# The four column-group matmuls of a product kept as one piece by a list scheduler

## The chip, the cores and the metric

The kernel runs on one core of one Trainium2 chip. The metric is the device time of one execution in microseconds (us), the median of several runs of the same built program.

## What is computed

One step of a hybrid decoder layer for two request groups that share weights: a prompt of 2048 tokens and eight decode tokens, each token a row of 1024 channels. Cut to what matters here:

```python
x = x + parallel_mixer(rms_norm(x, norm_mix), ...)       # convolution module and gated DeltaNet
x = x + memory_attend(rms_norm(x, norm_mem_q), mem_k, mem_v, w_mq, w_mo)
x = x + swiglu(rms_norm(x, norm_ffn), w_gate, w_up, w_down)
...
def memory_attend(h, mem_k, mem_v, w_mq, w_mo):
    q = (h @ w_mq).reshape(bsz, seq, MEM_HEADS, MEM_HD)
    s = jnp.einsum('blhd,bmhd->bhlm', q, mem_k) * (MEM_HD ** -0.5)
    pr = jax.nn.softmax(s, axis=-1)
    o = jnp.einsum('bhlm,bmhd->blhd', pr, mem_v)
    return o.reshape(bsz, seq, MEM_HEADS * MEM_HD) @ w_mo
```

The decode tokens have their own cached keys and values (8 tokens, 256 memory rows, 4 heads of 256). Everything is float32.

## The kernel before, in words

The prompt is worked in four blocks of 512 tokens: the mixer for all blocks first, then for each block the output projection, the memory attention (`sc` scores, `pr` probabilities, `rg` result) and the feed-forward part, whose products are `fx`, `fy`, `fz` (gate and up) and `dx`, `dy`, `dz`, `dn` (down). These prompt products use operands split into a high and a low part in float32r, three matmuls for each product, and fill TensorE's whole width of 128 columns.

The eight decode tokens ride along. Three of their products have few columns on the stationary side, 8 or 32, and are written in float32 without a split. Each of these matmuls writes 8 or 32 partitions of a PSUM bank, starting at partition 32 j, and so uses one of TensorE's four column groups; the helper `quad` issues one. Four of them with j = 0 to 3, on four different operands, make a group:

- `dr` (in `dec_rows`): a decode row times `w_mq` (operand `hdn`) or `w_mo` (operand `hcat`). The four stationary operands are four channel chunks of the row, the four moving ones four weight tiles `raw`, 128x512, loaded by DMA. A product of 512 columns takes two groups, each weight four: 8 groups, 32 matmuls.
- `podd` (in `dec_attend`): the probabilities `pb` times the cached values. The four moving operands are `vtd` tiles, two tokens by two halves of the memory rows. Two column halves with four groups each: 8 groups, 32 matmuls.

The decode scores come before that: a DVE or POOL multiplication `kt` = `kt` * `qb` and a DVE reduction into `scs`, 32 of each, while the prompt's third block is in its attention.

**What sets the order.** The program is first recorded: every engine call is put on a tape with its operands (`Tape.add`). `Tape.order` then makes the order in which the calls are issued, by list scheduling. It keeps a clock for each engine and for the DMA; `cost` gives each call a duration, `LAT` the delay between engines. `graph` finds for each call what it must follow (`preds`): who wrote its operands, who used its output before, and for PE the last PE call on the same PSUM tile. At each turn, the engine that is free first takes, among the calls that are ready by its clock, the one with the smallest key. For PE the key is the place on the tape; for the others it is the smallest key of what hangs on them (`keys`). A matmul with a later place is therefore taken when nothing earlier is ready at that moment, and the next turn chooses again. `tensor_tensor` calls in SBUF can go to DVE or POOL, whichever the planner finds free.

So in the kernel before, each of the four `quad` calls of a group is a call of its own: it is ready when its own operand has landed by the planner's clock and the call before it on the same bank is issued, and it competes with the `fx`, `fy` and `fz` rows for its turn. The planner's cost of one is `n * 0.4492 + 15` ns.

All calls of the tape are issued from one line (515 before, 530 after), so the profile tells them apart by tile names alone.

Of the kernel before, what the change touches and what calls it, by code (L numbers as in the profile page):

```python
# [8 lines left out]
F32 = mybir.dt.float32  # L9
# [71 lines left out]
class Clock:  # L81


    def __init__(self):
        self.at = {"pe": 0.0, "act": 0.0, "dve": 0.0, "pool": 0.0, "sp": 0.0, "dma": 0.0}
        self.ready, self.used = {}, {}
        self.table = None
        self.ring, self.nbank = {}, {"mm": 3, "s": 3, "o": 1, "cv": 1}
        self.held = set()
# [23 lines left out]
def elems(ap):  # L113
    n = 1
    for x in ap.shape[1:]:
        n *= x
    return n
# [37 lines left out]
class Tape:  # L155
# [10 lines left out]

    def __init__(self):
        self.ops, self.tag_of, self.bufs, self.psum = [], {}, {}, set()
        self.real, self.other, self.given = {}, {}, {}

    def pool(self, pool, bufs, psum=False):
        return TapePool(self, pool, bufs, psum)
# [16 lines left out]
    def cost(self, eng, op, args, kw, outs, ins):  # L189

        n = max(elems(a) for a in outs + ins) if ins else elems(outs[0])
        psum_in = any(a.name in self.psum for a in ins)
        if eng == "pe":
            m = elems(args[1])
            n = elems(args[2])
            if op == "transpose":
                return max(n, m) * 0.835 + 3, False, None
            if args[1].dtype == F32 and m <= 32 and n >= 256:
                return n * 0.4492 + 15, False, None
            if args[1].dtype == F32:  # L200
                return 2 * (max(max(m, 64) * 0.835, 2 * n * 0.4492) + 3), False, None
            return max(max(m, 64) * 0.835, (n if n >= 256 else 4 * n) * 0.4492) + 3, False, None
        if eng == "sp":
            size = 4
            for x in outs[0].shape:
                size *= x
            return max(size / 295.0, 90.0), False, None
        if eng == "act":
            ptr = len(ins) - 1
            return 0.834 * n + (50 if psum_in else 94) + 93 * ptr + (92 if "accum_out" in kw else 0), False, SETS.get(kw.get("func"))  # L210
        big = sum(a.name not in self.psum and elems(a) > 1 for a in ins)
        if eng == "dve":
            ptr = any(hasattr(kw.get(k), "shape") for k in ("scalar", "scalar1"))
            half = op in ("tensor_copy", "tensor_scalar") and not psum_in
            shared = big > 1 or (half and n > 2 and not any(a.name in self.psum for a in outs))
            return 68 + (61 if ptr else 0) + n * (6.2 if op == "reciprocal" else 0.525 if half else 1.042), shared, None
        if kw.get("op") == ALU.pow:
            return 280 + 180 * n, True, None
        if op in ("memset", "affine_select"):
            return 40 + 0.85 * n, False, None  # L220
        return 150 + n * (2.15 if op == "tensor_tensor" else 3.4), True, None

    def box(self, a):

        if a.name in self.psum:
            return 0, 0, 0, 0
        dims = a.ap
        shape = a.tensor.shape
        pitch = 1
        for x in shape[1:]:  # L230
            pitch *= x
        if a.space == bass.MemoryType.DRAM:
            pitch = shape[-1]
        r0, c0 = a.offset // pitch, a.offset % pitch
        r1, c1 = r0, c0
        for st, n in dims:
            if pitch > 1 and st % pitch == 0:
                r1 += st // pitch * (n - 1)
            else:
                c1 += st * (n - 1)  # L240
        if c1 >= pitch:
            r1, c0, c1 = r1 + c1 // pitch, 0, pitch - 1
        return r0, r1, c0, c1

    def graph(self):

        writes, reads, last_pe = {}, {}, {}
        preds, tiles = [], []
        over = lambda x, y: x[0] <= y[1] and y[0] <= x[1] and x[2] <= y[3] and y[2] <= x[3]
        inside = lambda x, y: y[0] <= x[0] and x[1] <= y[1] and y[2] <= x[2] and x[3] <= y[3]  # L250
        for n, (eng, op, _, args, _, outs, ins, _) in enumerate(self.ops):
            p = {}
            for a in ins:
                if a.name in self.tag_of:
                    b = self.box(a)
                    for k, x in writes.get(a.name, ()):
                        if over(b, x):
                            p[k] = 1
            for a in outs:
                if a.name in self.tag_of:  # L260
                    b = self.box(a)
                    for k, x in writes.get(a.name, ()):
                        if over(b, x):
                            p[k] = 1
                    for k, x in reads.get(a.name, ()):
                        if over(b, x):
                            p[k] = 1
                    if eng == "pe":
                        if a.name in last_pe:
                            p[last_pe[a.name]] = 1  # L270
                        last_pe[a.name] = n
            for a in outs:
                if a.name in self.tag_of:
                    b = self.box(a)
                    for d in (writes, reads):
                        d[a.name] = [(k, x) for k, x in d.get(a.name, ()) if not inside(x, b)]
                    writes[a.name].append((n, b))
            for a in ins:
                if a.name in self.tag_of:
                    reads.setdefault(a.name, []).append((n, self.box(a)))  # L280
            p.pop(n, None)
            preds.append(list(p))
            tiles.append(list(dict.fromkeys(a.name for a in outs + ins if a.name in self.tag_of)))
        return preds, tiles

    def keys(self, succs, line, first, tiles):


        N = len(self.ops)
        nxt = {}  # L290
        for tag, ts in line.items():
            for k, t in enumerate(ts[: -self.bufs[tag]]):
                nxt[t] = first[ts[k + self.bufs[tag]]]
        key = list(range(N))
        for n in range(N - 1, -1, -1):
            if self.ops[n][0] != "pe":
                after = [key[m] for m in succs[n]] + [key[nxt[t]] for t in tiles[n] if t in nxt and nxt[t] > n]
                key[n] = min([n + LATER, *after])
        return key

    def order(self):
# [69 lines left out]
        def taken(t):  # L371
            load = max(0.0, clock["dve"] - t)
            for _, m in avail["dve"]:
                if not gone[m]:
                    load += cost(m, "dve")[0]
            return load
# [11 lines left out]
        while len(done) < N:  # L388
# [20 lines left out]
            while av:  # L409
# [4 lines left out]
                if not busy and n in self.other:  # L414
                    load += cost(n, "dve")[0]
                    busy = load > BACKLOG
                    n = None
                    continue
# [14 lines left out]
                if stop is None:  # L433
                    if e == "dve" and cost(n, e)[1] and port_at > t + 150 and not skipped:

                        other = [(k2, m) for k2, m in av if not gone[m] and not cost(m, e)[1] and all(x in given for x in tiles[m]) and bank_at(m, e) <= t]
                        if other:
                            skipped.append((k, n))
                            k, n = min(other)
                            av.remove((k, n))  # L440
                            heapify(av)
                            new = []
                    break
# [194 lines left out]
def hybrid_step(ctx: ExitStack, tc: tile.TileContext, i: dict, o: list):  # L638
# [146 lines left out]
    class Plan(list):  # L785
# [21 lines left out]
        def extend(self, keys):  # L807
            for key in keys:
                self.append(key)
# [2321 lines left out]
```

## Time and profile before

| | |
|---|---|
| median of 3 runs | 2936.22 us (2935.59 to 2937.78) |
| profiled execution, its own time | 2932.24 us |
| its span, first to last instruction | 2930.5 us |
| mean granted TensorE clock | 0.998 |
| busy: PE, DVE, ACT, POOL | 2890.9, 2470.0, 1452.0, 754.0 us |
| DMA moved | 569.40 MB, 194 GB/s |

How to read the rows that follow in the prediction. A row of the groups gives engine, operation, output <- inputs, the shape of the stationary operand (partitions * columns), the output's shape, the number of records, then busy time in us, the mean of one in ns, and the idle time of the engine just before them. A row of the timeline gives start and length in us, then the same names; records of one kind that follow each other are merged, with their count; brackets hold an idle time before the row. The length reaches to the end of the last record, which overlaps the next start, so what a row takes from the engine is the difference of two starts. A float32 matmul leaves two records. A row of waits gives who waited for whom, us in total, times, and the longest. A row of windows gives the stretch, its length, the busy time of PE, weight loads, DVE, ACT and POOL, the granted clock, the DMA share and GB/s.

### The profile page before, as it was taken

How to read it: one execution, taken by the hardware profiler on the slowest of the kernel's cores; microseconds unless marked ns; L12 is line 12 of the kernel's file. 1: busy time of each engine (PE TensorE's matmuls, PEld its weight loads, DVE VectorE, ACT ScalarE, POOL GpSimd, SP SyncE). 2: the span in 40 equal slices, each digit the busy share in tenths (PEclk: the TensorE clock that was granted, in tenths of full speed). 3: DMA queues.
4: the chain of work that ended last, by engine and by line, in shares of the span. 5: the costliest groups of instructions: out<-in, count | busy, mean ns of one | idle time of the engine just before them, and what ended most of it. 6: DMA issues, size and time to landing. Idle time of an engine off the chain costs nothing.

```text
span 2930.5 us, 55769 instructions
## 1 busy us (share of the span) xinstructions
PE 2890.9 (99%) x19620; PEld 2598.0 (89%) x19620; DVE 2470.0 (84%) x5364; ACT 1452.0 (50%) x3034; POOL 754.0 (26%) x850
## 2 busy tenths in 40 slices
PE   9999999999999999999999999999999999999998
PEld 8999878888888887989888789999888999999998
DVE  8868988999978897978888877788867888888888
ACT  7544545555664445545454443344444444444444
POOL 3211342553313034613201810000542232410000
PEclk9999999999999999999999999999999999999999
DMA  6533435777774334866677767777636666666664
GB/s 222 155 97 105 128 115 162 228 247 258 225 243 124 119 102 133 261 192 201 213 259 251 246 217 246 232 232 238 201 102 207 210 214 199 209 230 197 214 209 131
DMA packets 363032, 569.40 MB, mean 194 GB/s; under 512 B 55840, under 2 KB 158560, under 8 KB 362736
## 3 DMA queue, kind: packets, MB, share of 16 engines
q1 hardware_dynamic: 362752, 565.84, 60.3%
q8 instruction: 155, 2.54, 0.3%
q14 instruction: 125, 1.02, 0.1%
HBM read 457.77 MB, written 108.51 MB: 193 GB/s over the span
## 4 chain that ended last, share of the span: by engine, by line
PE 51%; DVE 2%; DMA 2%; ACT 1%; issue 1%; POOL 0%; SPq 0%; POOLq 0%; DVEq 0%; ACTq 0%
PE fy L515 11%; PE fz L515 8%; PE fx L515 7%; PE rg L515 6%; PE dx L515 5%; PE dn L515 5%; PE dz L515 3%; PE sc L515 3%; PE dy L515 1%; DMA w<-sums 1%; DVE w L515 1%; PE pu L515 0%; PE podd L515 0%; DVE x L515 0%; PE pch L515 0%
## 5 line engine op out<-in xcount | busy, mean ns | idle before, releaser
L515 ACT ACTIVATE w<-raw 128x512 fp32r<-128x512 f32 (+1 forms) x1066 | 649.5, 619 | 888.9 <-issue 138.2
L515 DVE TENSOR_TENSOR w<-raw,w 128x512 fp32r<-128x512 f32 (+1 forms) x861 | 610.8, 713 | 161.5 <-ACT w L515 156.8
L515 PE MATMUL fy<-op,w 128*128 128x256 f32 (+1 forms) x3168 | 434.3, 282 | 0.1
L515 PEld LDWEIGHTS fy<-op,w 128*128 128x128 f32 x3168 | 399.1, 188 | 7.6 <-issue 1.8
L515 PE MATMUL hd<-hT,w 128*128 128x512 f32 (+2 forms) x1920 | 394.2, 356 | 1.0 <-DVE hT L515 0.5
L515 POOL TENSOR_TENSOR w<-raw,w 128x512 fp32r<-128x512 f32 (+1 forms) x205 | 282.5, 1382 | 341.7 <-ACT w L515 277.9
L515 DVE SCALAR_TENSOR_TENSOR cacc<-cu,cw,cacc 128x512 f32<-128x512 f32 x480 | 357.6, 745 | 9.2 <-ACT cacc L515 5.7
L515 PEld LDWEIGHTS hd<-hT,w 128*128 128x128 f32 x1920 | 302.6, 188 | 45.4 <-ACT w L515 1.2
L515 PE MATMUL fx<-op,w 128*128 128x256 f32 (+1 forms) x2112 | 297.3, 283 | 0.3
L515 PE MATMUL fz<-op,w 128*128 128x256 f32 (+1 forms) x2112 | 285.8, 283 | 1.8 <-DMA w<-sums 1.7
L515 PEld LDWEIGHTS fx<-op,w 128*128 128x128 f32 x2112 | 269.4, 189 | 8.3 <-ACT w L515 3.4
L515 PEld LDWEIGHTS fz<-op,w 128*128 128x128 f32 x2112 | 264.5, 188 | 9.0 <-issue 4.8
L515 PE MATMUL dx<-fo,w 128*128 128x256 f32 (+1 forms) x1344 | 197.8, 283 | 0.7 <-DVE x L515 0.6
L515 PE MATMUL rg<-pT,w 128*128 128x512 f32 x768 | 191.3, 400 | 2.1 <-ACT pr L515 0.9
L515 PE MATMUL dn<-ff,w 128*128 128x512 f32 (+2 forms) x960 | 192.0, 353 | 0.3 <-ACT ffs L515 0.2
L515 PE MATMUL sc<-w,hT 128*128 128x512 f32 x768 | 188.5, 399 | 3.6 <-ACT pr L515 3.6
L515 PE MATMUL rg<-catS,w 128*128 128x512 f32 (+2 forms) x960 | 186.2, 351 | 0.0
L515 PEld LDWEIGHTS dx<-fo,w 128*128 128x128 f32 x1344 | 174.7, 188 | 2.7 <-DVE x L515 1.3
L515 PEld LDWEIGHTS rg<-catS,w 128*128 128x128 f32 x960 | 154.6, 188 | 24.6
L515 PEld LDWEIGHTS sc<-w,hT 128*128 128x128 f32 x768 | 141.4, 188 | 36.8 <-ACT pr L515 5.9
L515 PEld LDWEIGHTS rg<-pT,w 128*128 128x128 f32 x768 | 140.5, 188 | 35.8 <-ACT pr L515 2.2
L515 PEld LDWEIGHTS dn<-ff,w 128*128 128x128 f32 x960 | 150.9, 188 | 22.0 <-DVE ffs L515 0.5
(421 smaller groups left out, 4836.6 us busy)
## 6 DMA issues: line engine op xcount, KB each, us to landing
w<-sums SPq DMA_DIRECT2D x222, 512.0 KB, 4.4
raw<-in_w_gate_dram SPq DMA_DIRECT2D x192, 256.0 KB, 3.5
sums<-w SPq DMA_DIRECT2D x66, 512.0 KB, 3.7
raw<-in_w_up_dram SPq DMA_DIRECT2D x118, 256.0 KB, 3.4
raw<-in_w_down_dram SPq DMA_DIRECT2D x224, 128.0 KB, 2.8
raw<-in_w_in_dram SPq DMA_DIRECT2D x96, 256.0 KB, 3.2
raw<-sums SPq DMA_DIRECT2D x74, 256.0 KB, 3.3
raw<-wk SPq DMA_DIRECT2D x64, 256.0 KB, 2.8
```

The source lines that it names most:

```text
L515: fn(*args, **kw)
```

## The change

The scheduler is told of the groups. A new function `quarter` says which PE calls are column-group matmuls (float32, at most 32 stationary columns, at least 256 moving ones). In `graph`, up to four such calls in a row on the same PSUM tile are a group: the first call of a group is given what the other three must follow too, so it isn't ready before all four operands are. In `keys`, the second to fourth have the length of the tape taken from their keys, so that, ready as soon as the one before is issued, they come ahead of everything else. The planner's cost of one such matmul rises from `n * 0.4492 + 15` to `n * 0.4492 + 38` ns. No instruction of the computation is added or removed; only the order changes, and with it which of DVE and POOL makes some sums.

```diff
@@ __init__ @@
-        self.real, self.other, self.given = {}, {}, {}
+        self.real, self.other, self.given, self.follow = {}, {}, {}, set()
@@ cost @@
-            if args[1].dtype == F32 and m <= 32 and n >= 256:
-                return n * 0.4492 + 15, False, None
+            if self.quarter(op, args):
+                return n * 0.4492 + 38, False, None
@@
+    def quarter(self, op, args):
+
+        return op == "matmul" and args[1].dtype == F32 and elems(args[1]) <= 32 and elems(args[2]) >= 256
@@ graph @@
-        preds, tiles = [], []
+        preds, tiles, group = [], [], []
...
             p.pop(n, None)
+            if eng == "pe" and self.quarter(op, args):
+                if group and group[0] == outs[0].name and len(group) < 5:
+                    preds[group[1]] = list(dict.fromkeys([*preds[group[1]], *(k for k in p if k < group[1])]))
+                    group.append(n)
+                    self.follow.add(n)
+                else:
+                    group = [outs[0].name, n]
+            elif eng == "pe":
+                group = []
             preds.append(list(p))
@@ keys @@
+        for n in self.follow:
+            key[n] -= N
         return key
```

What it does to the order is shown at three places. The first is PE in the feed-forward part of the second block, where the last group of the second `w_mq` product stands; `dr_3367` is its bank, `raw_...` the weight tiles, `fy` and `fx` rows of the prompt. Before:

```order
L515 MATMUL dr_3367_3566<-raw_3392_3591,hdn_104 8x512
L515 MATMUL dr_3367_3566<-raw_3393_3592,hdn_104 8x512
L515 MATMUL dr_3367_3566<-raw_3394_3593,hdn_104 8x512
L515 MATMUL fy_3401_3600<-op_2433_2632,w_3403_3602 128x256 x3
L515 MATMUL fy_3401_3600<-op_2445_2644,w_3403_3602 128x256 x3
L515 MATMUL fy_3401_3600<-op_2459_2658,w_3403_3602 128x256 x3
L515 MATMUL fy_3401_3600<-op_2482_2681,w_3403_3602 128x256 x3
L515 MATMUL dr_3367_3566<-raw_3395_3594,hdn_104 8x512
L515 MATMUL fx_3411_3610<-op_2430_2629,w_3410_3609 128x256 x6
```

After:

```order
L530 MATMUL dr_3367_3566<-raw_3392_3591,hdn_104 8x512
L530 MATMUL dr_3367_3566<-raw_3393_3592,hdn_104 8x512
L530 MATMUL dr_3367_3566<-raw_3394_3593,hdn_104 8x512
L530 MATMUL dr_3367_3566<-raw_3395_3594,hdn_104 8x512
L530 MATMUL fy_3401_3600<-op_2433_2632,w_3403_3602 128x256 x3
L530 MATMUL fy_3401_3600<-op_2445_2644,w_3403_3602 128x256 x3
L530 MATMUL fy_3401_3600<-op_2459_2658,w_3403_3602 128x256 x3
L530 MATMUL fy_3401_3600<-op_2482_2681,w_3403_3602 128x256 x3
L530 MATMUL fx_3411_3610<-op_2430_2629,w_3410_3609 128x256 x6
```

The fourth matmul has moved ahead of twelve `fy` rows. The second place is PE in the feed-forward part of the third block, where the last `podd` group of the first column half begins; `vtd_3871` to `vtd_3874` are its four value tiles. Before, three pieces, of which the last stands further on:

```order
L515 MATMUL podd_3772_3971<-vtd_3871_4070,pb_3716_3915 32x512
L515 MATMUL fz_3848_4047<-op_3730_3929,w_3835_4034 128x256 x3
L515 MATMUL fz_3848_4047<-op_3737_3936,w_3835_4034 128x256 x3
L515 MATMUL fz_3848_4047<-op_3747_3946,w_3835_4034 128x256 x3
L515 MATMUL fz_3848_4047<-op_3756_3955,w_3835_4034 128x256 x3
L515 MATMUL podd_3772_3971<-vtd_3872_4071,pb_3717_3916 32x512
L515 MATMUL fy_3853_4052<-op_3730_3929,w_3836_4035 128x256 x3
```

After:

```order
L530 MATMUL fz_3848_4047<-op_3756_3955,w_3835_4034 128x256 x3
L530 MATMUL fx_3841_4040<-op_3755_3954,w_3838_4037 128x256
L530 MATMUL podd_3772_3971<-vtd_3871_4070,pb_3716_3915 32x512
L530 MATMUL podd_3772_3971<-vtd_3872_4071,pb_3717_3916 32x512
L530 MATMUL podd_3772_3971<-vtd_3873_4072,pb_3716_3915 32x512
L530 MATMUL podd_3772_3971<-vtd_3874_4073,pb_3717_3916 32x512
L530 MATMUL fy_3853_4052<-op_3730_3929,w_3836_4035 128x256 x3
```

The first of the four has moved behind the `fz` rows, and the others stand right after it. In all, six of the sixteen groups were cut before, into pieces of 3 and 1 (two `dr` groups), 2 and 2 (two `podd` groups), 1, 1 and 2, and 2, 1 and 1; after the change all sixteen stand whole. The third place is POOL in the attention of the third block, around the power that makes the norm's scale `rs1_3606`; `kt` are the decode score products, `w` the low parts of weights. Before:

```order
L515 TENSOR_TENSOR w_3616_3815<-raw_3579_3778,w_3616_3815 128x512
L515 TENSOR_TENSOR kt_3600_3799<-kt_3600_3799,qb_3599_3798 128x512
L515 TENSOR_TENSOR rs1_3606_3805<-ms_3605_3804,ex_98 128x4
L515 TENSOR_TENSOR w_3623_3822<-raw_3589_3788,w_3623_3822 128x512
L515 TENSOR_TENSOR kt_3574_3773<-kt_3574_3773,qb_3573_3772 128x512
```

After:

```order
L530 TENSOR_TENSOR kt_3600_3799<-kt_3600_3799,qb_3599_3798 128x512
L530 TENSOR_TENSOR kt_3601_3800<-kt_3601_3800,qb_3599_3798 128x512
L530 TENSOR_TENSOR w_3616_3815<-raw_3579_3778,w_3616_3815 128x512
L530 TENSOR_TENSOR kt_3574_3773<-kt_3574_3773,qb_3573_3772 128x512
L530 TENSOR_TENSOR kt_3575_3774<-kt_3575_3774,qb_3573_3772 128x512
L530 TENSOR_TENSOR kt_3608_3807<-kt_3608_3807,qb_3607_3806 128x512
L530 TENSOR_TENSOR rs1_3606_3805<-ms_3605_3804,ex_98 128x4
L530 TENSOR_TENSOR kt_3609_3808<-kt_3609_3808,qb_3607_3806 128x512
```

Five operations stand between `kt_3600` and the power where none stood; behind it follow `kt` products as far as `kt_3639` in both orders, 23 on POOL in all for 22 before.

## The prediction

> **What bounds the kernel now.** I read the page first, then the list of TensorE's instruction groups, then TensorE's timeline around the small matmuls, then its waits and the DMA queue.
>
> ```profile
> span 2930.5 us, 55769 instructions
> PE 2890.9 (99%) x19620; PEld 2598.0 (89%) x19620; DVE 2470.0 (84%) x5364; ACT 1452.0 (50%) x3034; POOL 754.0 (26%) x850
> ```
>
> TensorE is busy in all but some 40 us of the span. So a microsecond of PE time that disappears is a microsecond of the whole, unless another engine then makes PE wait for it. The matmuls of the change are three groups:
>
> ```profile
> L515 PE MATMUL podd<-vtd,pb 128*32 128x512 f32 x64 | 14.8, 605 | 0.0
> L515 PE MATMUL dr<-raw,hdn 128*8 128x512 f32 x32 | 5.2, 594 | 0.0
> L515 PE MATMUL dr<-raw,hcat 128*8 128x512 f32 x32 | 5.2, 594 | 0.0
> ```
>
> Each matmul leaves two records, so these are 32, 16 and 16 matmuls: eight, four and four groups of four. What one group costs is read from the timeline. Call a run of them with nothing between a visit. A visit by a whole group, with plain matmuls (f*) after it:
>
> ```profile
> 1748.25 1.06 PE L515 MATMUL podd<-vtd,pb 128*32 128x512 f32 x8
> 1749.24 1.33 PE L515 MATMUL fx<-op,w 128*128 128x256 f32 x9
> 1750.41 1.58 PE L515 MATMUL fz<-op,w 128*128 128x256 f32 x12
> 1751.83 1.58 PE L515 MATMUL fy<-op,w 128*128 128x256 f32 x12
> ```
>
> All four (eight records) hold PE for 1749.24 - 1748.25 = 0.99 us; their busy union is 1.06 because ends overlap the next start. Twelve plain matmuls take 1751.83 - 1750.41 = 1.42 us. Now groups that are cut up:
>
> ```profile
> 1765.77 1.58 PE L515 MATMUL fy<-op,w 128*128 128x256 f32 x12
> 1767.28 1.05 PE L515 MATMUL podd<-vtd,pb 128*32 128x512 f32 x4
> 1768.26 1.69 PE L515 MATMUL fx<-op,w 128*128 128x256 f32 x12
> 1769.88 1.05 PE L515 MATMUL podd<-vtd,pb 128*32 128x512 f32 x2
> 1770.86 1.68 PE L515 MATMUL fz<-op,w 128*128 128x256 f32 x12
> 1772.47 1.05 PE L515 MATMUL podd<-vtd,pb 128*32 128x512 f32 x2
> 1773.44 1.69 PE L515 MATMUL fy<-op,w 128*128 128x256 f32 x12
> ```
>
> A visit of two matmuls (x4) holds PE for 0.98 us, a visit of one (x2) for 0.98 us, as long as a visit of four. Matmuls in different column groups run side by side, and whoever comes alone pays for all four. So cost goes by visits, not by matmuls. The busy times count them: 14.8 / 1.06 = 14 visits for eight groups, and each 5.2 / 1.04 = 5 visits for four, 24 visits where 16 would do. Eight are surplus, and nothing hides them, since PE is what the span is made of.
>
> **The change, part by part.**
>
> *Keeping the four together.* The order of the change shows all 16 groups whole. From one lone visit to the next is 1769.88 - 1767.28 = 2.60 and 1772.47 - 1769.88 = 2.59 us, and the twelve plain matmuls in it are worth 1.42. A surplus visit thus costs 1.17 us: 0.98 while it holds PE, and 0.2 by which the change to and from it stretches the neighbours. The other matrix agrees:
>
> ```profile
> 1558.60 1.04 PE L515 MATMUL dr<-raw,hdn 128*8 128x512 f32 x6
> 1559.57 1.70 PE L515 MATMUL fy<-op,w 128*128 128x256 f32 x12
> 1561.19 1.02 PE L515 MATMUL dr<-raw,hdn 128*8 128x512 f32 x2
> 1562.15 1.69 PE L515 MATMUL fx<-op,w 128*128 128x256 f32 x12
> ```
>
> 1561.19 - 1558.60 = 2.59 for a visit of three (0.97) and the twelve after it; the lone fourth holds PE 0.96. Eight visits at 1.17 are 9.4 us of PE. A whole group is 0.01 us longer than a lone visit (0.99 against 0.98), 0.06 for the six groups that were cut: nothing. The Trainium skill (TensorE: Matmul & The Clock Gate, Measured speedup vs the span model) speaks against a full gain: it has three column tiles run 2.38 times as fast as one after the other and four row tiles 3.07 times, so four together would take 4 / 3.07 = 1.3 times one alone. By that figure, an estimate, the six groups would give back up to 6 x 0.3 x 0.98 = 1.8 us and the sum would be 7.6; here the rows have three as long as one, and they decide.
>
> *The first waits for all operands.* Behind it, on PE's in-order queue, stands everything else that PE has. The last loads of the groups, from the SP queue:
>
> ```profile
> 1542.45 1.62 SPq L515 DMA_DIRECT2D raw<-in_w_mq_dram  x2
> 1748.40 2.32 SPq L515 DMA_DIRECT2D vtd<-in_cache_mem_v_dram  x5
> 1813.09 0.80 SPq L515 DMA_DIRECT2D vtd<-in_cache_mem_v_dram  x2
> 1837.79 2.10 SPq L515 DMA_DIRECT2D vtd<-in_cache_mem_v_dram  x2
> 1958.21 4.89 SPq L515 DMA_DIRECT2D raw<-in_w_mo_dram  x4
> DMA to landing us min/median/max: 2.8/4.5/7.5
> ```
>
> The last row is of the vtd tiles. The tightest is the first `podd` group that was cut: its first pair runs at 1760.44, its fourth operand leads the five issues from 1748.40 and so is there by 1748.40 + 7.5 = 1755.9 at the worst. The others have 10 us or more: 1542.45 + 1.62 against 1558.60 less a landing; 1813.09 against 1845.63; 1839.9 against 1865.83; 1963.1 against 1981.31.
>
> ```profile
> 1760.44 1.05 PE L515 MATMUL podd<-vtd,pb 128*32 128x512 f32 x4
> 1845.63 1.05 PE L515 MATMUL podd<-vtd,pb 128*32 128x512 f32 x4
> 1865.83 1.05 PE L515 MATMUL podd<-vtd,pb 128*32 128x512 f32 x4
> 1981.31 1.04 PE L515 MATMUL dr<-raw,hcat 128*8 128x512 f32 x6
> ```
>
> The loads keep their places on SP's queue to within two rows, and the slots of the `vtd` tiles, for which later loads wait there, come free when the group ends, not later than the last of its pieces did. I put the wait at 0. If it comes, it costs what the load slips; the bound is the 7.5 us of the slowest load, once.
>
> *The followers' keys and the new cost (38 for 15).* These issue nothing of their own, but the planner's clocks move, and with them plain rows of PE, DVE, POOL and SP from 1.47 to 2.05 ms. Swapping plain runs costs PE nothing by the rows above (1.42 us per twelve whichever comes first). What can change is PE's waits there. From 1570 to 1720 us, where the scores, the softmax and the decode rows' `kt` products meet, the longest is
>
> ```profile
> PE sc L515 <- ACT pr L515: 3.0, 2, 2.0
> PE fz L515 <- DMA w<-sums: 1.4, 2, 1.0
> ```
>
> 3.0 us in two waits; the second row, for 1550 to 2060, is the weight loads. The 3.0 may go or double, which bounds this term by -3 and +3; I take 0, since the same chain of tiles stands in both orders. Behind the last moved row, about 2.05 ms, the orders are equal on every engine.
>
> **The sum.** The profiled execution took 2932.2 us around its span of 2930.5, 4.0 less than the median of the runs. 2932.2 - 9.4 = 2922.8; against the median 2936.2 - 9.4 = **2926.8 us**, with 2923.8 to 2929.8 by the wait term alone. A measurement of this kernel tells about 0.2% (5.9 us) from no change, so "faster" means below 2930.3.
>
> **The rivals.**
>
> *A. The weight loads set the pace, and PE waits for what it saved.* For it:
>
> ```profile
> 1750.00:1760.00 10.00, 10.00 (x87) 10.00 (x87) 4.87 (x9) 4.66 (x8) 0.00 (x0) 1.00 0.96 356
> 1760.00:1770.00 10.00, 10.00 (x74) 7.92 (x73) 5.16 (x10) 3.49 (x7) 0.53 (x1) 1.00 0.96 333
> 1770.00:1780.00 10.00, 10.00 (x68) 7.51 (x67) 5.68 (x13) 4.17 (x8) 0.00 (x0) 1.00 0.71 211
> ```
>
> The DMA engines are at 0.96 for 20 us just where four visits go. Against it: they are at 0.71 in the next 10 us, so no backlog is left, and the issues are set free by PE's own progress. All six `podd` visits lost that way give 2926.8 + 6 x 1.17 = 2933.8, no change.
>
> *B. Slower: POOL's queue holds up the softmax.* In the changed order five POOL operations stand between `kt_3600` and the power that makes the scale `rs`, where none stood, and eight `kt` products follow on which DVE's in-order queue reduces before its last reciprocal; the exponentials that free PE's score banks stand behind both.
>
> ```profile
> L515 POOL TENSOR_TENSOR kt<-kt,qb x22: 1267/1332/1749, 1580.5 to 1680.1; 128x512 f32<-128x512 f32 x22
> 1651.49 0.15 DVE L515 TENSOR_SCALAR nrs<-rs 128x4 f32<-128x4 f32 x1
> 1665.02 1.22 DVE L515 TENSOR_SCALAR mx<-mx,nrs 128x2 f32<-128x2 f32 x2
> ```
>
> If all thirteen came late at the slowest product and PE idled for each, 13 x 1.75 = 22.8 us: 2926.8 + 22.8 = 2949.6. It decides from nine of them (15.3 us = 9.4 + 5.9). Against it: the scale is ready at 1651.64 and first used at 1665.02, 13.4 us of slack that swallow the first five (8.8), and the other eight alone (14.0) don't reach 15.3. The Trainium skill (TensorE: Matmul & The Clock Gate, What's actually happening) adds that an idle window of about 3.4 us halves PE's clock until it has been busy as long, an estimated 3.4 us more; no wait of this trace reaches that, and the granted clock is 1.00 in every window shown above.
>
> *C. The first of a group does wait.* A slip of about 3 us at two groups, inside the 7.5 bound: 2926.8 + 6 = 2932.8, no change.
>
> That the change doesn't do what it says is excluded: the order shows 16 whole groups, and whole groups ran at 0.99 us before.
>
> **How the numbers follow.** Forecast 0.76, A 0.14, B 0.04, C 0.06. The forecast's own spread stays just below 2930.3; I leave 0.02 of it in "same". Faster 0.74, same 0.22, slower 0.04. The range reaches from 2923 (both score waits gone is 2923.8; less the 0.6 us between the lowest run and the median) to 2934 (A), and leaves out B.
>
> **What would show it.** In the profile of the changed kernel, `podd` busy 8 x 1.06 = 8.5 us for 14.8 and each `dr` 4.2 for 5.2; every one of their rows in the timeline with x8; no wait of `podd` or `dr` on a DMA; `sc` waiting about 3 us, `w<-sums` under 3. Wrong would be: fewer visits and the same span, with PE idle before `fz` or `fx` (A) or `sc` (B).

## The result, and the profile after

| | before | after |
|---|---|---|
| median of 5 runs each, us | 2936.97 (2935.59 to 2943.57) | 2926.18 (2923.72 to 2932.57) |
| ratio, 95% interval | | 0.9961 (0.9945 to 0.9978) |
| profiled execution, us | 2932.24 | 2926.35 |
| its span, us | 2930.5 | 2924.3 |

The changed kernel is faster: 0.39% of 2936.97 is 11.5 us (6.5 to 16.2 by the interval). The forecast was 2926.8, and 9.4 us less. One execution of e4, an experiment below, took 5937.89 us, twice the time of its other five, and stands in no median or ratio here. The head of the page of after, and its groups of the column-group matmuls (line, engine, operation and tiles; then busy us and mean ns of one; then idle time ahead):

```profile
span 2924.3 us, 55772 instructions
PE 2884.1 (99%) x19620; PEld 2597.7 (89%) x19620; DVE 2470.5 (84%) x5365; ACT 1451.7 (50%) x3034; POOL 752.8 (26%) x849
L530 PE MATMUL podd<-vtd,pb 128*32 128x512 f32 x64 | 8.5, 605 | 0.0
L530 PE MATMUL dr<-raw,hdn 128*8 128x512 f32 x32 | 4.2, 594 | 0.0
L530 PE MATMUL dr<-raw,hcat 128*8 128x512 f32 x32 | 4.2, 594 | 0.0
```

The number of records and the mean of one are those of before; only the busy union has shrunk, since all four of a group now run side by side. 8.5 / 1.06 = 8 visits and twice 4.2 / 1.04 = 4: 16 for 24. TensorE's timeline of after, where before had one `podd` group in three pieces:

```profile
1767.60 1.57 PE L530 MATMUL fz<-op,w 128*128 128x256 f32 x12
1769.01 0.28 PE L530 MATMUL fx<-op,w 128*128 128x256 f32 x1
1769.21 1.06 PE L530 MATMUL podd<-vtd,pb 128*32 128x512 f32 x8
1770.21 1.68 PE L530 MATMUL fy<-op,w 128*128 128x256 f32 x12
```

One visit of 1770.21 - 1769.21 = 1.00 us does what took 2 x 2.6 us and a third visit before, with plain rows between.

Where the time went is read between two marks that both orders have, the first and the last `dr` group. Before:

```profile
1466.81 1.04 PE L515 MATMUL dr<-raw,hdn 128*8 128x512 f32 x8
...
2047.70 1.04 PE L515 MATMUL dr<-raw,hcat 128*8 128x512 f32 x8
```

After:

```profile
1470.17 1.04 PE L530 MATMUL dr<-raw,hdn 128*8 128x512 f32 x8
...
2038.56 1.04 PE L530 MATMUL dr<-raw,hcat 128*8 128x512 f32 x8
```

580.89 us became 568.39, 12.5 less. The visits forecast 9.4 of it. PE's waits in that stretch make up most of the rest. All rows of PE's waits there (who waited for whom: us in total, times, longest), before:

```profile
PE sc L515 <- ACT pr L515: 3.0, 2, 2.0
PE fz L515 <- DMA w<-sums: 1.4, 2, 1.0
PE pss L515 <- DVE sqj L515: 0.3, 1, 0.3
PE rg L515 <- ACT pT L515: 0.2, 1, 0.2
PE dn L515 <- ACT ffs L515: 0.2, 1, 0.2
```

After:

```profile
PE sc L530 <- ACT pr L530: 1.0, 1, 1.0
PE dx L530 <- DVE x L530: 1.0, 3, 0.5
PE rg L530 <- ACT pT L530: 0.2, 1, 0.2
PE fz L530 <- DMA w<-sums: 0.2, 1, 0.2
```

5.1 us became 2.4. No column-group matmul waits for a load. 9.4 + 2.7 = 12.1 of the 12.5.

The span fell by only 6.2, because this execution of after lost 3.4 us ahead of the first mark (1470.17 - 1466.81) and 2.9 behind the last (885.7 for 882.8 us to the end), where the orders of the two kernels are equal on every engine. 2.6 of the 3.4 stand in one place, read against before, whose matmuls there are the same. The timeline of before, and then of after (in brackets, PE's idle time ahead and who ended it):

```profile
823.10 1.63 PE L515 MATMUL vp<-w,kvT 128*128 128x512 f32 x6
826.15 1.67 PE L515 MATMUL vp<-w,kvT 128*128 128x512 f32 x6 [1.42 <-ACT jn L515]
827.75 1.10 PE L515 MATMUL pu<-u,W 64*128 64x64 f32 x8
```

```profile
823.46 1.63 PE L530 MATMUL vp<-w,kvT 128*128 128x512 f32 x6
827.83 2.93 PE L530 MATMUL vp<-w,kvT 128*128 128x512 f32 x6 [2.74 <-ACT jn L530]
830.69 1.25 PE L530 MATMUL pu<-u,W 64*128 64x64 f32 x8
```

The wait for ScalarE's evacuation `jn` is 1.3 us longer, and behind it six records take 2.93 us for 1.67. The windows view of after says why (length; busy us of PE, PEld, DVE, ACT and POOL with their counts; then granted clock, DMA share, GB/s):

```profile
827.60:831.00 3.40, 3.17 (x8) 2.13 (x8) 0.69 (x1) 1.01 (x3) 0.00 (x0) 0.50 0.99 378
```

The granted clock was 0.50 for 3.4 us. The orders are equal there, so the change doesn't explain it. It comes back below: such stretches make single executions of one kernel differ.

### The profile page after: what moved, and what is told of

It is laid out like the page before. It is cut to its first block, busy times and chain, and to the rows that moved or that the text cites. A ratio compares the mean times of both kernels' runs of the same rounds, so it can differ in the third digit from the quotient of the medians.

```text
span 2924.3 us, 55772 instructions
## 1 busy us (share of the span) xinstructions
PE 2884.1 (99%) x19620; PEld 2597.7 (89%) x19620; DVE 2470.5 (84%) x5365; ACT 1451.7 (50%) x3034; POOL 752.8 (26%) x849
## 4 chain that ended last, share of the span: by engine, by line
PE 86%; DVE 7%; DMA 3%; ACT 2%; issue 1%; SPq 0%; POOL 0%; DVEq 0%; POOLq 0%; ACTq 0%
PE fy L530 12%; PE rg L530 11%; PE hd L530 11%; PE fz L530 8%; PE fx L530 8%; PE dn L530 6%; PE dx L530 5%; PE sc L530 5%; PE dz L530 3%; PE glua L530 2%; PE glub L530 2%; PE pu L530 2%; DVE cacc L530 2%; PE mkv L530 1%; PE pch L530 1%
```

## The experiments

My theory: the time goes with the number of visits, some 1.17 us each, whatever sets that number. The rivals: the gain comes from the new plan (the cost of 38, other waits) and not from the visits; or the joint wait of the first does the work, for good or ill. Each ratio is to the kernel before on the same chip, with its 95% interval; the microseconds are one less the ratio, times that chip's median of before (2935.80 to 2939.65). Visits are counted in the instruction order. The last column is the time from the first to the last `dr` group in the one profiled execution of each, read as above; e3 has no whole groups, so it has none. Row by row, by tile names in the traces, e4 and e9 ran the same order as the change on every engine, and e8 the same as e2.

| kernel | visits | median, us | ratio | us less than before | first to last `dr`, us |
|---|---|---|---|---|---|
| e3, each matmul alone | 64 | 2989.38 | 1.0173 (1.0155 to 1.0191) | -50.9 | |
| before | 24 | 2936.97 | 1 | 0 | 580.89 |
| e8, joint wait alone | 24 | 2937.08 | 0.9998 (0.9988 to 1.0008) | 0.6 | 579.27 |
| e2, cost alone | 24 | 2936.39 | 0.9991 (0.9979 to 1.0003) | 2.6 | 579.27 |
| e7, `dr` groups alone | 22 | 2932.73 | 0.9993 (0.9982 to 1.0003) | 2.1 | 575.12 |
| e6, `podd` groups alone | 18 | 2930.02 | 0.9981 (0.9969 to 0.9993) | 5.6 | 572.37 |
| e1, old plan, groups joined afterwards | 16 | 2931.51 | 0.9972 (0.9959 to 0.9985) | 8.2 | 574.22 |
| e9, the change again | 16 | 2932.47 | 0.9971 (0.9960 to 0.9982) | 8.5 | 569.02 |
| the change | 16 | 2926.18 | 0.9961 (0.9945 to 0.9978) | 11.5 | 568.39 |
| e5, the change with the old cost | 16 | 2924.74 | 0.9957 (0.9941 to 0.9972) | 12.6 | 568.36 |
| e4, early keys alone | 16 | 2925.87 | 0.9952 (0.9935 to 0.9970) | 14.1 | 568.42 |

**e1: nothing but the visits.** The plan of before is kept to the row; afterwards the followers are moved up behind the first of their group.

```diff
-            for n in self.order():
+            for n in self.joined(self.order()):
+    def joined(self, done):
...
+        after = {g[0]: g[1:] for g in groups}
+        late = {n for g in groups for n in g[1:]}
+        return [m for n in done if n not in late for m in (n, *after.get(n, ()))]
```

> The plan of the kernel before, with one thing done behind it: the second to fourth matmul of each group are taken from their places and put right behind the first. 16 visits, the old cost, every other row on every engine as before. Visits theory: 8 x 1.17 = 9.4 us less than before (ratio 0.9968), podd busy 8.5 us and each dr 4.2. Plan theory (the gain is from the new cost and the rows that moved with it, in the attention above all): no change, 0.999 to 1.001.

It is 8.2 us faster (4.4 to 12.1), for 9.4 by the sum. Its groups of instructions have `podd` with 8.5 busy and each `dr` with 4.2:

```profile
L532 PE MATMUL podd<-vtd,pb 128*32 128x512 f32 x64 | 8.5, 605 | 0.0
```

Between 1570 and 1720 us its PE waits hold the score wait of before, unchanged:

```profile
PE sc L532 <- ACT pr L532: 3.0, 2, 2.0
```

Between the marks it gains only 6.7 us (574.22 for 580.89). Behind the score wait its clock was at one half, and in before, behind the same wait, it wasn't. The window in e1:

```profile
1677.50:1680.90 3.40, 3.40 (x12) 2.60 (x11) 3.02 (x6) 0.87 (x2) 3.08 (x3) 0.50 0.11 33
```

The same rows in the timeline of e1, and then of before:

```profile
1675.99 2.08 PE L532 MATMUL sc<-w,hT 128*128 128x512 f32 x7 [1.99 <-ACT pr L532]
...
1681.83 0.38 PE L532 MATMUL ppt<-ident,pr 128*128 128x128 f32 x2
```

```profile
1675.74 1.90 PE L515 MATMUL sc<-w,hT 128*128 128x512 f32 x7 [1.97 <-ACT pr L515]
...
1680.03 0.38 PE L515 MATMUL ppt<-ident,pr 128*128 128x128 f32 x2
```

They take 5.84 us in e1 and 4.29 in before: the half clock cost 1.6. With that taken off, and 0.3 us of longer waits in the stretch (5.4 for 5.1), the eight visits are worth some 8.5 us there, an estimate: 1.1 each.

So whole groups without a new plan bring nearly what the visits cost, and the wait that the changed kernel lost belongs to the new plan.

**e2: the cost alone.** In the kernel before, one number.

```diff
-                return n * 0.4492 + 15, False, None
+                return n * 0.4492 + 38, False, None
```

> The kernel before with the planner's cost of a column-group matmul at 38 for 15, and no groups. The order still has 24 visits, but rows of the attention move. Visits theory: no change beyond what PE's waits in the attention do, -3 to +3 us (0.999 to 1.001). Plan theory: 6 to 10 us faster.

No clear difference (-0.9 to 6.2 us), and the groups stay cut: its `podd` row has 14.8 busy and its `dr` rows 5.2 each, as before. e8, the same order again, has 0.6 (-2.3 to 3.5), which leaves the 6 to 10 of the plan theory out.

The score wait moved all the same: in the same window it has 1.1 us, and a new wait of 1.4 beside it. The planner's numbers shuffle waits of a microsecond; they don't join groups.

```profile
PE ppt L515 <- DVE pr L515: 1.4, 1, 1.4
PE sc L515 <- ACT pr L515: 1.1, 1, 1.1
```

**e3: more visits, not fewer.** No column-group matmul may follow another within 500 ns of plan time, and each is costed at what a lone visit takes, so that all 64 stand alone.

```diff
-                return n * 0.4492 + 38, False, None
+                return n * 2.29, False, None
...
+                if e == "pe" and self.quarter(self.ops[n][1], self.ops[n][3]) and t < alone[0]:
+                    ready[n] = alone[0]
...
+            if e == "pe" and self.quarter(self.ops[n][1], self.ops[n][3]):
+                alone[0] = fin + 500.0
```

> The changed kernel with the scheduler told that a column-group matmul may not follow another within 500 ns of its clock, and that each costs a whole 1.17 us: 64 visits of one matmul each. Visits theory: 40 visits more than before, 40 x 1.17 = 46.8 us slower than before (ratio 1.0159), podd busy 32 x 1.06 = 33.9 us and each dr 16 x 1.04 = 16.6. If a visit's cost goes by its matmuls (the skill's 3 column tiles at 2.38 times one after the other give four at most 1.3 times one), single ones are cheaper than visits of four and the loss is under 40 us. Plan theory: within 3 us of before.

It is 50.9 us slower (45.6 to 56.1): 40 more visits at 1.27 us each (1.14 to 1.40). Its groups, from its page:

```profile
L538 PE MATMUL podd<-vtd,pb 128*32 128x512 f32 x64 | 33.5, 605 | 0.0
L538 PE MATMUL dr<-raw,hdn 128*8 128x512 f32 x32 | 16.4, 594 | 0.0
```

33.5 / 32 = 1.05 and 16.4 / 16 = 1.03 us for a lone visit, where a whole group has 1.06 and 1.04. Its timeline:

```profile
1771.27 1.04 PE L538 MATMUL podd<-vtd,pb 128*32 128x512 f32 x2
1772.24 0.86 PE L538 MATMUL fx<-op,w 128*128 128x256 f32 x5
1773.03 1.05 PE L538 MATMUL podd<-vtd,pb 128*32 128x512 f32 x2
1774.01 0.74 PE L538 MATMUL fx<-op,w 128*128 128x256 f32 x4
```

**e4 and e8: which half of the change joins the groups.** e4 is the changed kernel without the joint wait, e8 without the early keys of the followers. The line that each leaves out of the changed `graph`:

```diff
e4:
-                    preds[group[1]] = list(dict.fromkeys([*preds[group[1]], *(k for k in p if k < group[1])]))
e8:
-                    self.follow.add(n)
```

> The changed kernel without the joint wait: the first of a group is given nothing of the others to wait for, the followers keep their early keys. The order still has 16 visits. Visits theory: as the changed kernel, 9 to 10 us less than before (ratio 0.9965, +-0.001). If the joint wait is what brings the gain, it goes back toward before (0.998 to 1.0).

> The changed kernel without the early keys: the first of a group waits for all four operands, the followers compete as before. The order still has 24 visits, in the same pieces as with the new cost alone. Visits theory: as the new cost alone (0.998 to 1.0). If the joint wait helps by itself: as the changed kernel (0.996).

With the keys alone all 16 groups are whole, and the time is 14.1 us less (8.8 to 19.1). With the wait alone all 24 visits remain, and so does the time (0.6, from -2.3 to 3.5). The `podd` row of e8:

```profile
L529 PE MATMUL podd<-vtd,pb 128*32 128x512 f32 x64 | 14.8, 605 | 0.0
```

A follower whose operands are there still loses to a plain row with an earlier key; only its own key keeps it at the group. In this kernel the joint wait moves no row: e4 ran the order of the change without it, and e8 ran the order of e2 with it. The operands are there anyway: in e4 too no `podd` or `dr` waits for a load.

**e5: the change with the old cost.** 38 becomes 15 again.

```diff
-                return n * 0.4492 + 38, False, None
+                return n * 0.4492 + 15, False, None
```

> The changed kernel with the planner's cost back at 15. 16 visits. Visits theory: 9.4 us less than before, give or take 3 us of PE's waits (ratio 0.9958 to 0.9978). Cost theory (the truer cost brings part of the gain): clearly less gain than the changed kernel, ratio over 0.998.

12.6 us less (8.2 to 17.3), with 16 visits: the cost isn't needed either.

**e6 and e7: one kind of group alone.** Only `podd` (32 columns), or only `dr` (8), is joined; the other kind keeps the new cost and its own keys.

```diff
e6:
-            if eng == "pe" and self.quarter(op, args):
+            if eng == "pe" and self.quarter(op, args) and elems(args[1]) == 32:
e7:
-            if eng == "pe" and self.quarter(op, args):
+            if eng == "pe" and self.quarter(op, args) and elems(args[1]) < 32:
```

> The changed kernel with groups for podd alone; dr's calls stay single. 18 visits, the new cost. Visits theory: 6 x 1.17 = 7.0 us less by visits, with the 2 to 3 us less waiting that the new cost alone brought about 9.5 (ratio 0.9967, +-0.001); podd busy 8.5, dr 5.2 each.

> The changed kernel with groups for dr alone. 22 visits, the new cost. Visits theory: 2 x 1.17 = 2.3 us less by visits, about 5 with the waits of the new cost (ratio 0.998 to 0.999); podd busy 14.8, dr 4.2 each.

e6 gains 5.6 us (2.1 to 9.1) where I expected about 9.5; its six visits are worth 7.0. e7 gains 2.1 (-0.9 to 5.3) where I expected about 5; its two visits are worth 2.3. Both miss by their medians. Between the marks e6 gains 8.5 and e7 5.8, near what I expected. The score wait of e7 is 1.0, but the waits for the weights' low parts rose from 1.4 to 2.1, so that PE's waits in the stretch come to 3.3 for 5.1:

```profile
PE fz L530 <- DMA w<-sums: 2.1, 2, 1.1
PE sc L530 <- ACT pr L530: 1.0, 1, 1.0
```

So by the stretch a part of the change brings its visits and some of the waits; the medians of these two runs are too coarse to show it.

**e9: the changed kernel once more,** to see how much of the differences among 16-visit kernels is scatter. Its code is that of after.

> The changed kernel once more, on the same chip as the next one. 9 to 12 us less than before (ratio 0.996 to 0.997) by visits and shorter waits. In this and other profiles PE's granted clock is at half for single stretches of 3.4 us after it has waited 1.5 us or more near 660, 830 and 1270 us, and not the same ones in each execution; if these make the scatter of the runs, this profile's span minus 1.7 us for each stretch lies within 1.5 us of the first profile of this kernel treated in the same way.

Ratio 0.9971 for 0.9961: the intervals overlap, and 8.5 against 11.5 us is scatter, and so is e4's 14.1 for the same order. Its profiled span is 2930.8, 6.5 longer than the first. Between the marks it is only 0.6 longer; 4.3 of the 6.5 stand ahead of them and 1.6 behind. The windows of e9 have the clock at one half for two double stretches:

```profile
829.00:835.80 6.80, 6.80 (x27) 5.91 (x26) 2.68 (x6) 3.85 (x9) 0.00 (x0) 0.50 0.89 322
1265.90:1272.70 6.80, 6.80 (x28) 5.92 (x28) 2.24 (x6) 1.66 (x4) 0.40 (x2) 0.50 0.39 112
```

13.6 us at half clock, against 6.8 in the first profile (one of its stretches stands above, the other begins near 647 us). Half of the difference is 3.4 us at most, and 3.1 of the 6.5 stay unexplained, twice what I had allowed: a miss. The expectation's "1.5 us or more" and "single stretches of 3.4 us" don't hold either: these two are double, and the last section has a stretch behind a wait of 1.11 us.

**e10: a version that takes less time than both.** The longest waits that are left belong to `wk` and `vp`, which wait for ScalarE's evacuations `jn`; they also stand ahead of the half-clock stretch at 828 us. Here every other `jn` is made on VectorE.

```diff
+    turn = [0]
...
-        if scale is None:
+        turn[0] += 1
+        if turn[0] % 2:
+            if scale is None:
+                V.tensor_copy(out=y, in_=pt)
+            else:
+                V.tensor_scalar(out=y, in0=pt, scalar1=scale, scalar2=None, op0=ALU.mult)
+        elif scale is None:
             A.activation(out=y, in_=pt, func=AF.Copy)
...
```

> The changed kernel, and the evacuations jn of the products wk and vp alternate between ScalarE and VectorE where all were ScalarE's. PE waited 4.2 us (wk) and 5.0 us (vp) for jn in the changed kernel's profile, the longest 2.7 us, with a stretch of half clock behind it. If ScalarE's queue is what PE waited for: these waits fall below 3 us in all, no half stretch near 830 us, 5 to 9 us less than the changed kernel (ratio to before 0.993 to 0.995). If VectorE's queue is as full there (it is at 0.8 to 1.0), the wait changes its name and the time stays within 2 us of the changed kernel.

Median 2924.28 us, ratio 0.9945 (0.9931 to 0.9958), 16.2 us less than before. Beside it on the same chip e9, the changed kernel, took 2932.47: its nine executions lie between 2926.14 and 2935.16, the six of e10 between 2921.47 and 2926.65, and the intervals of the two ratios don't touch. That of e4, which has the order of the change, reaches to 0.9935 and does hold e10's ratio. The waits of the first profile of the changed kernel, over the whole span:

```profile
PE wk L530 <- ACT jn L530: 4.8, 5, 1.2
PE vp L530 <- ACT jn L530: 4.6, 3, 2.7
```

The expectation had 4.2 and 5.0 for these. And two of the three for `jn` that are left in e10:

```profile
PE wk L530 <- DVE jn L530: 1.6, 1, 1.6
PE wk L530 <- ACT jn L530: 1.2, 1, 1.2
```

With the third, of `vp`, they come to 3.9 for 9.4, not quite the under 3 expected. The granted clock is 1.00 from 820 to 840 us, where e9 and the first profile dropped to one half. But the profiles of before, e1 and e2, with every `jn` on ScalarE, have 1.00 from 800 to 840 us too, so it isn't shown that the shorter waits keep the clock up. What of the gain is the shorter wait and what the clock I have not separated. e10 still has 6.8 us at half clock later on, from 1258.5 us.

## Why the prediction was right

**The visits: right, and shown.** e1 changes them and nothing else, and gives 8.2 us for 9.4. Over all kernels the time follows the count: the five with 16 visits are 11.0 us below before on average, the three with 24 (before, at 0, among them) 1.1; 9.9 us for 8 visits is 1.24 each, and e3 gives 1.27 going the other way. The price of 1.17 lies inside e3's interval (1.14 to 1.40), if at the low side. Between the marks, with the difference in PE's waits taken off, a visit is worth some 1.1 us from before to e1 (its half clock taken off too), and 1.1 to 1.2 from e8 to e4 and from e2 to the change, estimates from single profiles.

**The number: in part luck.** 2926.8 for 2926.18 is nearer than the working can claim. The same order had a median of 2932.47 in e9, and the sum left out 2.7 us of waits.

**A whole group costs as much as a lone matmul: right.** 1.00 us in the timeline of after; in e3 a lone visit has a busy union of 1.05 and 1.03, in after a whole one 1.06 and 1.04. The 1.3 times that I had taken from the Trainium skill (TensorE: Matmul & The Clock Gate, Measured speedup vs the span model) isn't seen. The same section's span model, one matmul and about 4 ns for each further tile, does agree: 0.98 + 3 x 0.004 = 0.99 by it, an estimate.

**The joint wait at 0: right.** No `podd` or `dr` waits for a load in after, and with or without the joint wait the order is the same (e4, e8).

**PE's waits at 0: mis-sized.** I kept the two score waits at 3.0 us. They fell to 1.0 and, with the smaller ones, PE's waits in the changed stretch fell by 2.7: inside the bound of 3 that I had set, and on the side that brings more gain. e1 keeps the 3.0 and gains less (8.2 for 11.5), as it should; but the intervals of the two overlap, so that the medians don't prove this term. Between the marks e1 is 5.8 us longer than after: 3.0 of it are PE's waits (5.4 for 2.4), 1.6 the half clock behind one of them, and 1.2 stay open.

**Rival A (weight loads): did not come.** The waits of `fz` for `w<-sums` in the stretch fell from 1.4 to 0.2 us. e7 shows that such a wait can rise, to 2.1.

**Rival B (POOL's queue and the softmax): did not come.** The scale and its first use in the timeline of after:

```profile
1655.09 1.04 DVE L530 TENSOR_SCALAR nrs<-rs 128x4 f32<-128x4 f32 x1
1666.27 1.46 DVE L530 TENSOR_SCALAR mx<-mx,nrs 128x2 f32<-128x2 f32 x2
```

It starts 3.6 us later than before, but 3.4 of these this execution had lost ahead of the first mark; counted from there the five POOL operations delay it by 0.2. It takes 1.04 us for 0.15, and by the same count its first use comes 2.1 us earlier. It still ends 10.1 us before that use, for 13.4 before: the slack was hardly needed.

**The clock: wrong beyond the windows shown.** The prediction said that no wait of this trace is long enough to halve the clock. The profile of before has such a stretch, in a part that I had not looked at:

```profile
647.20:650.60 3.40, 3.40 (x11) 2.53 (x10) 3.40 (x6) 0.23 (x1) 1.44 (x1) 0.50 1.05 405
```

The 3.4 us that the prediction put on a halved clock is too much as well: e1 shows 1.6 for such a stretch. None of this moved the forecast or a chance, since the change doesn't touch that part. But it bears on how near a single profile comes to a median.

**Open:** the differences of 8 to 14 us among the kernels with 16 visits. Three of them (the change, e4, e9) ran one and the same order, so 8.5 to 14.1 is scatter, and their stretches agree within 0.7 us. e5 has another plan and the same stretch. Only e1's stretch is longer, as said above. What makes the rest of the span differ from one execution to the next is explained in part by the half clock and otherwise not known.

## What to carry to other kernels

Small matmuls in different column groups cost by the visit: count the runs of them in TensorE's timeline, not their busy share, and price a surplus run by the distance from one to the next, less the work between. A list scheduler keeps such a group together through the keys of its followers; waiting for all operands at the head does not do it, and a better cost doesn't either. When 10 us of a 3 ms program are at stake, compare a stretch between two common marks in the traces, since the rest of the span can give back half of it by scatter. Here three profiles of one order agreed within 0.7 us on the stretch, while their gains by median ran from 8.5 to 14.1.

## What the runs showed of the hardware

The granted clock fell to 0.50 for 3.4 us, or 6.8, or once 10.2 (e8, from 829.5 us), behind waits of PE some of which were far shorter. The timeline of before, at the stretch quoted last:

```profile
645.70 1.10 PE L515 MATMUL pu<-u,W 64*128 64x64 f32 x8 [1.11 <-DVE u L515]
646.73 3.86 PE L515 MATMUL glub<-hT,w 128*128 128x512 f32 x9
650.84 1.41 PE L515 MATMUL glub<-hT,w 128*128 128x512 f32 x5
```

Nine records take 3.86 us here and five at full clock 1.41. Length alone doesn't decide: 1.11 us was followed by the drop here, and 1.42 at 826 us of the same execution by none. The score wait quoted with e1 was followed by the drop there, at 1.99 us, and in before, at 1.97 us, by none. The Trainium skill (TensorE: Matmul & The Clock Gate, What's actually happening) has the clock halved after an idle window of about 3.4 us, and that window running free of the program; the length of the stretches agrees, and so does their change from one execution to the next, but a whole idle window was not needed. A stretch costs at most half of its 3.4 us, an estimate from the 0.50; e1 shows 1.6. What in a wait brings one on was not tried.
